# Two query tiles taken through the chunks as they are normalized, and token rows moved behind the queries

## The chip, the cores and the metric

The kernel runs on one core of a Trainium2 chip. The metric is the device time of one execution in microseconds; three runs of the kernel before were timed. Engines: TensorE (PE; PEld is its weight load), VectorE (DVE), ScalarE (ACT), GpSimd (POOL) and SyncE (SP), which here only issues transfers.

## What is computed

One decoder layer over 512 tokens of width 2048, in float32:

```
xn = rmsnorm(x, norm_mix);  proj = xn @ w_in            # 80 tiles of 128 columns
y_conv = (gated 3-tap convolution) @ w_conv_out
y_attn = stick-breaking attention (16 heads of 64) @ w_attn_out
x = x + (sigmoid(g_conv)*y_conv + sigmoid(g_attn)*y_attn) @ w_out
xn = rmsnorm(x, norm_ffn)
q = xn @ peer_wq                                        # 16 tiles of 128 columns
scores = q . subkeys; top 16 of each half; top 16 of the sums -> 128 experts a token
x = x + sum_k gelu(xn . u[k]) * gate[k] * v[k]
out = rmsnorm(x, norm_final)
```

## The kernel before

**Precision.** Each product of two float32 operands is made of three matmuls: both operands are split into a high part (`whi`, ScalarE, L130) and a low part (`wlo`, VectorE, L131), and `mm3` (L160) adds high·high, high·low and low·high. Weights come as halves of 128x1024 (`whalf`, L139): a transfer by SP into one of four raw buffers, then a split into one of three high and three low buffers. The pace of TensorE is therefore tied to one split on ScalarE and one on VectorE for each half.

**Halves.** The tokens are taken in two halves of 256 (h = 0 and 1): projections, attention and gates (`mixer`), then the output projection with the residual (`outproj`, L450), then the second norm (`chain`, L490), then the queries (`queries`, L527). The expert part of the first 192 tokens is done row by row: for each of 128 slots a token row of u is fetched with an indirect transfer on POOL (`fetch`, L690) and multiplied on VectorE (L701, 128x2048), later the same with v (L708). The other 320 tokens are done densely against all 16384 experts (`dense`), which is most of the second half of the time.

**outproj** has two column halves of eight steps `kp`; each step takes two weight halves for both token tiles. After a column half, VectorE adds the residual (L483) and ScalarE squares the sum (L484), once for each of the two token tiles.

**chain** makes the norm's factor of each token tile (`rms_inv`: L194 adds the two sums, L195 takes the root on ScalarE, L196 inverts), spreads it over the partitions (L498, a matmul at L499, L502), and then goes through eight chunks of two 128-column blocks each: four transposes (`turn`, L205), two scalings on VectorE (L508), and a split into high and low parts of the normalized x (`yhi`/`ylo` in the first half, `dxhi`/`dxlo` in the second). In the first half it then also makes the token rows that the row-by-row part needs: it loads the gain row, scales both token tiles in place (L517, 128x2048) and stores them, and stores the part of x that the dense stage needs. In the second half it loads that part back.

**queries** computes 16 tiles: 48 matmuls each, a copy (L536) and two small products with the sub-keys (L538). In the second half it begins in the program when `chain` has ended.

**Order.** The program is written with generators: work on the side (routing, one-hot gates, row fetches) is advanced between the steps of the main work by `background` (L965) with a rate per step; `pump` (L911) issues that many rows. A planner then orders the instructions of each engine by a timeline of its own, so an instruction that is ready early may move ahead of earlier ones. `keep_in_program_order` forbids one instruction to move ahead of what was traced before it on its engine; the products at L701 and L708 are pinned so. An output step that yields "end" is not given side work (only the last step of the second half in the kernel before); `pump(SKIPEND * RATE_O)` then issues 1.6 rows after the chain. PSUM has three banks named `pj` (accumulators, also used by the transposes), two double banks `z`, and one bank `tr`.

Of the kernel before, what the change touches and what calls it, by code (L numbers as in the profile page):

```python
# [53 lines left out]
XKB = 3  # L54
# [26 lines left out]
def block_kernel(ctx, tc, a, out, dbg=None):  # L81
# [117 lines left out]
    def turn(x2, k, pin):  # L199

        tp = accum()
        for kk in range(2):
            for tt in range(2):
                o = kk * NH + tt * P
                t = nc.tensor.transpose(tp[:, o:o + P], x2[tt][:, (k + kk) * P:(k + kk) * P + P], ident)  # L205
                if pin:
                    behind(t)
        return tp.rearrange("p (k t) -> p k t", k=2)
# [241 lines left out]
    def outproj(pool, h, m, box):  # L450
# [5 lines left out]
        for half in range(2):  # L456
            zt = [ztile() for _ in range(2)]
            for kp in range(8):
# [16 lines left out]
                if half == 1 and kp == 7 and h:  # L475
                    if PRE1:
# [4 lines left out]
            for tt in range(2):  # L481
                hs = slice(half * 1024, half * 1024 + 1024)
                nc.vector.tensor_tensor(x2[tt][:, hs], zt[tt], x2[tt][:, hs], OP.add)  # L483
# [6 lines left out]
    def chain(pool, h, box, nhi, nlo, c0):  # L490

        x2 = box["x2"]
        ib = accum()
# [8 lines left out]
        nc.scalar.copy(inv, ib[:, 0:NH])  # L502
        yield
        for k in range(0, KD, 2):
            tp = turn(x2, k, h == 0 and PINT)
# [3 lines left out]
            split(xk, nhi[:, k:k + 2, c0:c0 + NH], nlo[:, k:k + 2, c0:c0 + NH])  # L509
            yield  # L510
        if h == 0:
            grow = row()
            nc.sync.dma_start(grow, a["norm_ffn"].broadcast_to([P, D]))
            yield
            for tt, rn in enumerate(rns):
                xn = x2[tt]
                nc.vector.scalar_tensor_tensor(xn, xn, rn, grow, OP.mult, OP.mult)  # L517
                stop = min(tt * P + P, G0)
                nc.sync.dma_start(xn2d[tt * P:stop], xn[0:stop - tt * P])
                yield  # L520
            nc.sync.dma_start(ntd[0], nhi[:, :, G0:].bitcast(F32))
            nc.sync.dma_start(ntd[1], nlo[:, :, G0:].bitcast(F32))
        else:
# [3 lines left out]
    def queries(pool, h, st, nhi, nlo, c0):  # L527

        for half in range(2):
            zt = [ztile() for _ in range(2)]  # L530
            for cg in range(8):
                ct = half * 8 + cg
                acc = accum()[:, :NH]
                yield from mmk(acc, wtile(a["wq"][ct]), lambda k: nhi[:, k, c0:c0 + NH], lambda k: nlo[:, k, c0:c0 + NH])
# [451 lines left out]
    for what in queries(sm, 0, st, *n0, 0):  # L986
        background("half", 0)
    for what in ahead:
# [7 lines left out]
    with tc.tile_pool(name="cp", bufs=1, side="right") as cp:  # L996
        for _ in chain(cp, 1, box[1], *st["dense_x"], ND - NH):
            pass
# [3 lines left out]
    for what in queries(sm, 1, st, *st["dense_x"], ND - NH):  # L1002
# [94 lines left out]
```

## Time and profile before

| | us |
|---|---|
| median of three runs | 3612.64 (3610.05 to 3616.29) |
| profiled execution | 3619.12 |
| its span | 3617.4 |
| TensorE busy | 3513.1 |
| VectorE busy | 2831.2 |
| ScalarE busy | 1616.3 |
| POOL busy | 659.3 |

The span is what the profile covers of the profiled execution. Starts are microseconds from its beginning. In a timeline row, the first two numbers are start and duration, and a bracket at the end gives how long the engine was idle before the instruction and whose end released it. In a row of stretches, each engine has its busy time and, in brackets, its number of instructions; PEclk is the granted clock of TensorE (1.00 is 2.4 GHz, 0.50 is 1.2 GHz). The names of the tiles: `z` and `pj` are PSUM, `row` a token row of 128x2048, `wlo`/`whi` split weights, `sg` a scaled chunk, `ssq` the sums of squares.

### The profile page before, as it was taken

Reading aid. Unit: us, or ns where it says so; the run is one execution under the profiler, and the core shown is the slowest. Engines: PE = TensorE matmul, PEld = TensorE weight load, DVE = VectorE, ACT = ScalarE, POOL = GpSimd, SP = SyncE. Lnnn points to the kernel's source line nnn. Section 1 sums busy time; section 2 is a strip of 40 time slices with the busy share of each in tenths; the row PEclk is TensorE's granted clock in tenths of the full one; section 3 lists DMA queues with packets and bytes.
Section 4 is the critical chain, followed back from the end, with each engine's and each line's share of the span. In section 5 each row is a group of like instructions: output and inputs, shape, how many; then the busy total and the mean of one; then the engine's idle time right before and its main releaser. Section 6 shows DMA issues by size and latency. Waiting matters only on the chain.

```text
span 3617.4 us, 63262 instructions
## 1 busy us (share of the span) xinstructions
PE 3513.1 (97%) x25347; PEld 3410.4 (94%) x25347; DVE 2831.2 (78%) x4022; ACT 1616.3 (45%) x2275; POOL 659.3 (18%) x520
## 2 busy tenths in 40 slices
PE   9999999999999999889999999999999999999998
PEld 8999998898888999779999999999999999999998
DVE  6565557559987878788999886888887878888886
ACT  6454445445555534544337773333333333333334
POOL 0000000001233322112131111221122322322220
PEclk9999999999999999999999999999999999999999
DMA  6556555654788889898888889899988988899884
GB/s 204 180 178 225 187 187 196 208 184 137 260 348 309 335 332 346 322 331 335 298 327 319 311 315 365 329 356 338 339 328 328 346 330 333 327 346 343 328 329 162
DMA packets 292920, 1049.29 MB, mean 290 GB/s; under 512 B 35921, under 2 KB 105169, under 8 KB 238673
## 3 DMA queue, kind: packets, MB, share of 16 engines
q1 hardware_dynamic: 237328, 642.56, 50.5%
q0 software_dynamic: 55296, 402.68, 28.7%
q8 instruction: 199, 3.26, 0.4%
q14 instruction: 97, 0.79, 0.1%
HBM read 996.57 MB, written 47.97 MB: 289 GB/s over the span
## 4 chain that ended last, share of the span: by engine, by line
PE 59%; DMA 5%; DVE 4%; issue 2%; ACT 1%; POOL 0%; SPq 0%; ACTq 0%; DVEq 0%; POOLq 0%
PE pj L163 10%; PE pj L161 10%; PE pj L162 10%; PE z L161 9%; PE z L162 9%; PE z L163 9%; DVE wlo L131 2%; DMA wraw<-in_w_in 2%; PE pj L673 2%; DMA row<-in_u,idx 1%; DVE row L701 1%; ACT whi L130 1%; PE z L439 1%; DMA row<-in_v,idx 0%; DMA wraw<-in_w_mix 0%
## 5 line engine op out<-in xcount | busy, mean ns | idle before, releaser
L130 ACT ACTIVATE whi<-wraw 128x1024 fp32r<-128x1024 f32 x827 | 874.1, 1059 | 1258.0 <-PE pj L162 723.2
L131 DVE TENSOR_TENSOR wlo<-wraw,whi 128x1024 fp32r<-128x1024 f32 x827 | 1008.3, 1223 | 412.5 <-ACT whi L130 405.6
L161 PE MATMUL pj<-xhi,whi 128*128 128x256 f32 x2560 | 723.5, 283 | 12.5 <-ACT whi L130 10.3
L163 PE MATMUL pj<-xhi,wlo 128*128 128x256 f32 x2560 | 720.4, 283 | 13.5 <-DVE wlo L131 13.4
L162 PE MATMUL pj<-xlo,whi 128*128 128x256 f32 x2560 | 718.1, 281 | 0.0
L161 PE MATMUL pj<-dxhi,whi 128*128 128x320 f32 (+1 forms) x2304 | 710.0, 308 | 4.5 <-ACT whi L130 4.3
L163 PE MATMUL pj<-dxhi,wlo 128*128 128x320 f32 (+1 forms) x2304 | 703.6, 307 | 3.4 <-DVE wlo L131 3.3
L162 PE MATMUL pj<-dxlo,whi 128*128 128x320 f32 (+1 forms) x2304 | 705.2, 306 | 0.0
L161 PE MATMUL z<-ahi,whi 128*128 128x320 f32 x2048 | 632.0, 310 | 3.9 <-ACT z L190 2.9
L162 PE MATMUL z<-alo,whi 128*128 128x320 f32 x2048 | 631.8, 309 | 2.4 <-DVE alo L131 2.4
L163 PE MATMUL z<-ahi,wlo 128*128 128x320 f32 x2048 | 630.6, 309 | 1.8 <-DVE wlo L131 1.8
L163 PEld LDWEIGHTS pj<-xhi,wlo 128*128 128x128 f32 x2560 | 481.6, 189 | 23.6 <-DVE wlo L131 20.9
L161 PEld LDWEIGHTS pj<-xhi,whi 128*128 128x128 f32 x2560 | 482.5, 188 | 21.1 <-ACT whi L130 14.4
L690 POOL DMA_INDIRECT row<-in_v,idx x192 | 292.7, 1525 | 1060.2 <-DVE row L708 429.8
L162 PEld LDWEIGHTS pj<-xlo,whi 128*128 128x128 f32 x2560 | 482.3, 188 | 2.8 <-issue 1.6
L708 DVE SCALAR_TENSOR_TENSOR row<-row,gact 128x2048 f32<-128x2048 f32 x192 | 450.3, 2345 | 27.2 <-DMA row<-in_v,idx 27.2
L701 DVE SCALAR_TENSOR_TENSOR row<-row,gx 128x2048 f32<-128x2048 f32 x192 | 438.3, 2286 | 31.2 <-DMA row<-in_u,idx 31.1
L690 POOL DMA_INDIRECT row<-in_u,idx x192 | 289.0, 1505 | 863.1 <-DVE row L701 239.9
L161 PEld LDWEIGHTS pj<-dxhi,whi 128*128 128x128 f32 x2304 | 434.3, 189 | 5.5 <-ACT whi L130 5.1
L163 PEld LDWEIGHTS pj<-dxhi,wlo 128*128 128x128 f32 x2304 | 432.9, 188 | 5.4 <-DVE wlo L131 5.4
L162 PEld LDWEIGHTS pj<-dxlo,whi 128*128 128x128 f32 x2304 | 434.0, 188 | 0.0
L130 ACT ACTIVATE whi<-spare 128x1024 fp32r<-128x1024 f32 x197 | 208.8, 1060 | 425.4 <-PE z L162 266.9
(232 smaller groups left out, 4979.8 us busy)
## 6 DMA issues: line engine op xcount, KB each, us to landing
wraw<-in_w_in SPq DMA_DIRECT2D x320, 512.0 KB
wraw<-in_uT SPq DMA_DIRECT2D x187, 512.0 KB
wraw<-in_vT SPq DMA_DIRECT2D x128, 512.0 KB
spare<-in_vT SPq DMA_DIRECT2D x128, 512.0 KB
spare<-in_uT SPq DMA_DIRECT2D x69, 512.0 KB
wraw<-in_w_mix SPq DMA_DIRECT2D x64, 512.0 KB
wraw<-in_w_out SPq DMA_DIRECT2D x64, 512.0 KB
wraw<-in_wq SPq DMA_DIRECT2D x64, 512.0 KB
```

Source lines behind the costliest of these rows:

```text
L130: nc.scalar.activation(hi, src, AF.Copy)
L131: nc.vector.tensor_tensor(lo, src, hi.bitcast(F32), OP.subtract)
L161: nc.tensor.matmul(acc, shi, mhi, start=first, stop=False)
L162: nc.tensor.matmul(acc, shi, mlo, start=False, stop=False)
L163: pe_last[0] = nc.tensor.matmul(acc, slo, mhi, start=False, stop=last)
L439: nc.tensor.matmul(z[:, c], stat.bitcast(F32), src[:, c], start=False, stop=True, skip_group_check=True)
L673: behind(nc.tensor.matmul(gp[:, t * P:t * P + P], oh[:, t, 0], oh[:, t, 1], start=True, stop=True))
L690: ins = nc.gpsimd.indirect_dma_start(out=g, out_offset=None, in_=tab, in_offset=bass.IndirectOffsetOnAxis(ap=idx[0:np_, s:s + 1], axis=0))
L701: pin(nc.vector.scalar_tensor_tensor(g, g, 1.0, gx, OP.mult, OP.mult, accum_out=hid[:, s:s + 1]))
L708: pin(nc.vector.scalar_tensor_tensor(acc[0:np_], g, act[:, s:s + 1], acc[0:np_], OP.mult, OP.add))
```

## The change

1. The second half's queries are given the chain as a generator. They take two accumulators and, for each chunk that the chain has normalized, run the matmuls of the first two query tiles on that chunk; weight halves are requested for both tiles at a time. Then they go on as before from the third tile.
2. In the second half the transposes are made two chunks ahead, the first two before the norm's factor; they alternate between a `pj` bank and the bank `tr`, and the norm's spread uses a `z` bank.
3. The last four output steps of the second half (`CALM = 4`) yield "end", so no rows and no side work are issued there; at the last one ScalarE's square root table is loaded ahead. The two residual adds of the last column half are pinned in program order.
4. In the first half, the token rows, their stores and the store of the dense part leave `chain` for `norm_rows`, which is advanced while the queries run (after the first, fourth and sixth yield); the two scalings are pinned there.
5. The second half's scaled chunk has two buffers for three (`XKB`).

```diff
+CALM = 4
-XKB = 3
+XKB = 2
-    def turn(x2, k, pin):
-        tp = accum()
+    def turn(x2, k, pin, bank=None):
+        tp = accum() if bank is None else bank
...
-                if half == 1 and kp == 7 and h:
-                    if PRE1:
+                if half == 1 and kp >= 8 - CALM and h:
+                    if kp == 7:
                         tc.keep_in_program_order(nc.scalar.preload_act_table_set("sqrt_and_others"))
                     yield "end"
...
-                nc.vector.tensor_tensor(x2[tt][:, hs], zt[tt], x2[tt][:, hs], OP.add)
+                add = nc.vector.tensor_tensor(x2[tt][:, hs], zt[tt], x2[tt][:, hs], OP.add)
+                if h and half:
+                    tc.keep_in_program_order(add)
...
-        ib = accum()
+        tps = {}
+        def ahead_turn(k):
+            if k < KD:
+                bank = trtile() if h and k % 4 else None
+                tps[k] = turn(x2, k, h == 0 and PINT, bank)
+        if h:
+            ahead_turn(0)
+            ahead_turn(2)
+        ib = ztile() if h else accum()
...
         for k in range(0, KD, 2):
-            tp = turn(x2, k, h == 0 and PINT)
+            if h == 0:
+                ahead_turn(k)
+            tp = tps.pop(k)
...
             split(xk, nhi[:, k:k + 2, c0:c0 + NH], nlo[:, k:k + 2, c0:c0 + NH])
+            if h:
+                ahead_turn(k + 4)
             yield
...
+    def norm_rows(box, nhi, nlo):
+        nc.sync.dma_start(ntd[0], nhi[:, :, G0:].bitcast(F32))
+        nc.sync.dma_start(ntd[1], nlo[:, :, G0:].bitcast(F32))
+        grow = row()
+        nc.sync.dma_start(grow, a["norm_ffn"].broadcast_to([P, D]))
+        yield
+        for tt, rn in enumerate(box["rns"]):
+            xn = box["x2"][tt]
+            tc.keep_in_program_order(nc.vector.scalar_tensor_tensor(xn, xn, rn, grow, OP.mult, OP.mult))
+            stop = min(tt * P + P, G0)
+            nc.sync.dma_start(xn2d[tt * P:stop], xn[0:stop - tt * P])
+            yield
+    def queries(pool, h, st, nhi, nlo, c0, ch=None):
+        if ch is not None:
+            two = [accum()[:, :NH] for _ in range(2)]
+            next(ch)
+            for c in range(2):
+                ws = [whalf(a["wq"][ct, c]) for ct in range(2)]
+                for k in range(8 * c, 8 * c + 8):
+                    if k % 2 == 0:
+                        next(ch)
+                    for acc, (whi, wlo) in zip(two, ws):
+                        b = slice(k % 8 * P, k % 8 * P + P)
+                        mm3(acc, whi[:, b], wlo[:, b], nhi[:, k, c0:c0 + NH], nlo[:, k, c0:c0 + NH], k == 0, k == KD - 1)
+            for _ in ch:
+                pass
+            yield "two"
...
-    for what in queries(sm, 0, st, *n0, 0):
+    rest = norm_rows(box[0], *n0)
+    for i, what in enumerate(queries(sm, 0, st, *n0, 0)):
         background("half", 0)
+        if i in (0, 3, 5):
+            next(rest)
...
-        for _ in chain(cp, 1, box[1], *st["dense_x"], ND - NH):
-            pass
+        second = queries(sm, 1, st, *st["dense_x"], ND - NH, chain(cp, 1, box[1], *st["dense_x"], ND - NH))
+        next(second)
```

## Rows read from the trace of the kernel before

**Rows 1.** The page's busy time, share of the span and instructions, TensorE.
```profile
PE 3513.1 (97%) x25347; PEld 3410.4 (94%) x25347; DVE 2831.2 (78%) x4022; ACT 1616.3 (45%) x2275; POOL 659.3 (18%) x520
```

**Rows 2.** Busy time by stretch: stretch, length, engines, granted clock, share of DMA, GB/s.
```profile
730.00:812.00 82.00, 82.00 (x702) 82.00 (x702) 43.38 (x98) 35.43 (x46) 0.00 (x0) 1.00 0.53 173
...
1540.00:1590.60 50.60, 49.96 (x231) 40.54 (x230) 36.31 (x47) 25.50 (x37) 8.39 (x6) 1.00 0.93 348
1590.60:1607.30 16.70, 7.11 (x38) 5.49 (x37) 14.97 (x28) 9.49 (x17) 2.68 (x2) 0.80 1.03 331
...
1620.00:1712.00 92.00, 92.00 (x766) 92.00 (x765) 78.59 (x124) 37.63 (x48) 24.61 (x15) 1.00 0.92 347
...
2900.00:3000.00 100.00, 100.00 (x684) 100.00 (x683) 83.03 (x86) 35.99 (x45) 25.11 (x17) 1.00 0.87 333
```

**Rows 3.** Timeline of TensorE, last output matmul to first query matmul.
```profile
1590.21 0.39 PE L163 MATMUL z<-whi,xlo 128*128 128x512 f32 x1
...
1603.11 0.63 PE L205 MATMUL pj<-ident,row 128*128 128x128 f32 x4 [0.22 <-DVE sg L508]
1605.10 0.63 PE L205 MATMUL pj<-ident,row 128*128 128x128 f32 x4 [1.36 <-DVE sg L508]
...
1607.27 0.36 PE L161 MATMUL pj<-dxhi,whi 128*128 128x256 f32 x1 [0.15 <-DVE sg L508]
```

**Rows 4.** Timeline of VectorE in the second half's chain.
```profile
1590.62 1.22 DVE L131 TENSOR_TENSOR wlo<-wraw,whi 128x1024 fp32r<-128x1024 f32 x1
1591.75 1.22 DVE L483 TENSOR_TENSOR row<-z,row 128x1024 f32<-128x1024 f32 x1
1592.89 2.28 DVE L701 SCALAR_TENSOR_TENSOR row<-row,gx 128x2048 f32<-128x2048 f32 x1
...
1595.09 0.15 DVE L194 TENSOR_TENSOR ssq<-ssq 128x1 f32<-128x1 f32 x1
...
1598.64 0.16 DVE L196 RECIPROCAL ssq<-ssq 128x1 f32<-128x1 f32 x1
1600.53 2.44 DVE L508 SCALAR_TENSOR_TENSOR sg<-pj,gffn,cinv 128x256 f32<-128x256 f32 x6 [1.73 <-ACT cinv L502]
...
1610.41 1.47 DVE L131 TENSOR_TENSOR dxlo<-sg,dxhi 128x512 fp32r<-128x512 f32 x2
```

**Rows 5.** Timeline of ScalarE in the second half's chain and queries.
```profile
1593.00 1.03 ACT L484 ACTIVATE z<-row 128x1024 f32<-128x1024 f32 x1 [0.17 <-DVE row L483]
...
1594.17 1.28 ACT L195 ACT_TABLE_LOAD   x1
...
1596.48 0.29 ACT L195 ACTIVATE ssq<-ssq,epst 128x1 f32<-128x1 f32 x1 [0.72 <-DVE ssq L194]
...
1598.83 0.40 ACT L498 ACTIVATE rb<-ones,ssq 128x128 f32<-128x128 f32 x1 [1.76 <-DVE ssq L196]
...
1601.43 0.63 ACT L130 ACTIVATE dxhi<-sg 128x512 fp32r<-128x512 f32 x1 [0.94 <-DVE sg L508]
...
1626.54 0.35 ACT L536 COPY pq<-pj 128x256 f32<-128x256 f32 x1
...
1632.74 0.35 ACT L536 COPY pq<-pj 128x256 f32<-128x256 f32 x1
```

**Rows 6.** Busy time by stretch, second half's chain, for the granted clock.
```profile
1594.00:1595.00 1.00, 0.00 (x0) 0.00 (x0) 1.00 (x1) 0.98 (x3) 0.00 (x0) 0.72 1.24 260
...
1601.00:1607.00 6.00, 3.54 (x24) 2.36 (x22) 6.00 (x15) 3.15 (x5) 0.00 (x0) 0.98 1.00 408
```

**Rows 7.** Timeline of TensorE, end of the first half's chain.
```profile
710.48 0.39 PE L162 MATMUL pj<-ylo,whi 128*128 128x256 f32 x1 [1.82 <-DVE ylo L131]
...
712.50 0.35 PE L161 MATMUL pj<-yhi,whi 128*128 128x256 f32 x1 [1.16 <-DVE sg L508]
```

**Rows 8.** Timeline of VectorE, end of the first half's chain.
```profile
705.22 4.61 DVE L517 SCALAR_TENSOR_TENSOR row<-row,ssq 128x2048 f32<-128x2048 f32 x2
709.75 0.68 DVE L131 TENSOR_TENSOR ylo<-sg,yhi 128x512 fp32r<-128x512 f32 x1
```

More of the change, by code (lines that the diff above doesn't have):

```diff
@@ L502, in chain @@
         nc.scalar.copy(inv, ib[:, 0:NH])
+        box["rns"] = rns
         yield
         for k in range(0, KD, 2):
-            tp = turn(x2, k, h == 0 and PINT)
+            if h == 0:
+                ahead_turn(k)
+            tp = tps.pop(k)
             xk = pool.tile([P, 2, NH], F32, name="sg", bufs=1 if h == 0 else XKB)
@@ L509, in chain @@
             split(xk, nhi[:, k:k + 2, c0:c0 + NH], nlo[:, k:k + 2, c0:c0 + NH])
+            if h:
+                ahead_turn(k + 4)
             yield
[L511 to L523, printed above, removed]
+        if h:
             nc.sync.dma_start(nhi[:, :, 0:c0].bitcast(F32), ntd[0])
             nc.sync.dma_start(nlo[:, :, 0:c0].bitcast(F32), ntd[1])
-    def queries(pool, h, st, nhi, nlo, c0):
+    def norm_rows(box, nhi, nlo):
[25 more added lines that the diff above has]
+            yield "two"
         for half in range(2):
@@ L532, in queries @@
                 ct = half * 8 + cg
-                acc = accum()[:, :NH]
-                yield from mmk(acc, wtile(a["wq"][ct]), lambda k: nhi[:, k, c0:c0 + NH], lambda k: nlo[:, k, c0:c0 + NH])
+                if ch is not None and ct < 2:
+                    acc = two[ct]
+                else:
+                    acc = accum()[:, :NH]
+                    yield from mmk(acc, wtile(a["wq"][ct]), lambda k: nhi[:, k, c0:c0 + NH], lambda k: nlo[:, k, c0:c0 + NH])
                 pq = pool.tile([P, NH], F32, name="pq", bufs=2)
@@ L984, in background @@
             pump(rate)
-    for what in queries(sm, 0, st, *n0, 0):
+    rest = norm_rows(box[0], *n0)
+    for i, what in enumerate(queries(sm, 0, st, *n0, 0)):
         background("half", 0)
+        if i in (0, 3, 5):
+            next(rest)
+    for _ in rest:
+        pass
     for what in ahead:
@@ L1001, in block_kernel @@
     st["scp"] = small.enter_context(tc.tile_pool(name="scp", bufs=1))
-    for what in queries(sm, 1, st, *st["dense_x"], ND - NH):
+    for what in second:
         background(what, RATE_Q)
```

## Prediction

> **What bounds the kernel now.** I read the page first: TensorE is busy for 97% of the span [rows 1], so time can only be won where TensorE stands idle or is waiting on one chain, and everything else is cover. The busy time by stretch then says where that is. Once the last two thirds are running it is 100.00 of 100 us, with VectorE at 83% beside it; the two stretches that the change touches are not like that [rows 2]. In the last 50.6 us of the second output projection TensorE lacks only 0.6 us, so there is nothing to be had inside it. In the 16.7 us behind it TensorE works 7.1 us and VectorE 15.0.
>
> The timelines say why. Second half: TensorE's last output matmul ends at 1590.6 and the first query matmul starts at 1607.27 [rows 3]. VectorE in between is in a queue of its own making [rows 4]: the second residual add waits behind a weight split (1590.62) and starts only at 1591.75, and two token-row products of 2.28 us stand ahead of the root-mean-square steps: L194 of the first token tile runs only at 1595.09, when the first product ends, and L196 of the second at 1598.64, when the other one ends. On ScalarE a table load of 1.28 us lies in the same place [rows 5]. The first chunk's scaling starts at 1600.53. First half: the chain there is hidden beside projections, but TensorE waits 1.82 and 1.16 us for the sixth and seventh chunk [rows 7], since two token-row scalings (L517, together 4.61 us at 705.22) run ahead of the sixth chunk's low part at 709.75 [rows 8].
>
> **The change, part by part.** All sums are made against the profiled execution, 3619.12 us with a span of 3617.4; the median of the three timed runs is 3612.64, so I work out a difference there and take it from the median.
>
> *First half: token rows behind the queries.* L517 no longer stands ahead of the chunks, since it is issued after the second and third query tile and pinned there. VectorE then does the sixth chunk's low part at 705.2 instead of 709.75, the seventh chunk by 708.1 and the eighth by 709.5 (about 0.8 for its two scalings, 0.63 for the high part, 0.68 for the low one [rows 4, 5, 8]). TensorE needs them at 708.7, where it stopped, and then one each 0.7 us. Both waits go: **3.0 us**. The next wait would be the second weight half's low part, split at 708.9 to 710.1 once VectorE is free, and covered by the remaining chunks. In its new place L517 stands in a stretch where VectorE works 43 of 82 us and TensorE is never idle; products of the same length already stand in the second half's queries at no TensorE idle time (92.00 of 92) [rows 2]. So 0 there; without that cover 4.6. The two stores to the dense rows and the gain row's load move with it, behind the last chunk on SP's queue, where they also stood before; the weight loads queued behind them are four buffers ahead. I take 0. Bounds: -1 (the planner puts other filler there, and more of it) to 3.0 us, all that was idle.
>
> *Second half: no gathers in the last four output steps.* Three steps more than before issue no row (the last one issued none already), 2.4 rows at 0.8 a step. A product runs one or two steps of 5.6 us behind its request, so with none requested in the last 22 us the two products in the chain, 2 x 2.28, are gone. Table load: issued at the last output step, in a stretch where ScalarE works half of the time (25.5 of 50.6 [rows 2]), so 1.28 is hidden; if not, it stands before the square root as it does now. I follow the chain with the intervals of before. Add of the second token tile ends at 1592.9 (I leave the weight split ahead of it, since no pin forbids it). The square and its read-out take 1.16 (1593.00 to the table load at 1594.17); then come L194 (0.15), the square root (0.29) and L196 (0.16), with 0.1 to 0.2 of handing over before each: some 2.05 from the start of the square to the broadcast. From the broadcast (1598.83) to the first scaling (1600.53) it is 1.70 [rows 4, 5]. First scaling: 1593.05 + 2.05 + 1.70 = 1596.8, **3.7 us earlier**. Without the split ahead of the add it would be 1595.7.
>
> *Second half: two query tiles with the chunks.* Scaling to high part is 0.90, the high part 0.63, the low part behind it 0.7: the first chunk is usable at about 1599.0. From there TensorE owes two query tiles, 6.20 us each (from one query copy to the next [rows 5], the small sub-key products in it), and transposes: eight of the 32 run ahead in the wait for the norm and four more before the first chunk is split; the other twenty are five groups of 0.63 [rows 3]. 1599.0 + 12.4 + 3.15 = 1614.55. VectorE is not later: eight chunks took 11.35 us (1600.53 to 1611.88), and with three weight splits of 1.22 it is done at 1611.8 [rows 4]. Two things I add. The granted clock: some 3.7 us into the idle time it fell to 1.2 GHz, and from 1601 on it was 2.4 again [rows 6]. If the same happens now, the matmuls from 1599.0 to about 1601.6 go at half speed: 1.3 us (0 to 2). And the weight buffers: three are there for four halves, so the fourth is converted only when the first is free, 1.06 + 1.22 of conversion against 0.7 of the other tile's matmuls and 0.63 of transposes: 1.0 us. End of both tiles 1616.85. Before it is 1607.27 + 12.4 = 1619.67. **2.8 us gained**, less than the 3.7 that the norm gains, because before the queries of the first tile already started before the last two chunks were done. Bounds: +6.2 (no split ahead of the add, no clock loss, no buffer wait) to the loss under the rivals.
>
> *What is put off.* The 2.4 rows come later, in the even pacing of the long last stage: 2.4 x 2.36 = 5.7 us of VectorE spread over some 1300 us where TensorE lacks nothing [rows 2]. I take 0; the whole 5.7 if that cover were gone. The smaller edits (two buffers for the scaled chunk for three, the broadcast in another PSUM pool, the pinned adds) move no work; 0 each, with -1 to +1 for what they do to the planner's order.
>
> Sum: 3.0 + 2.8 = 5.8 us; 3617.4 - 5.8 = 3611.6 of span, and from the median 3612.64 - 5.8 = **3606.8 us**.
>
> **A rule against it.** In the second half's old chunk loop TensorE worked in bursts of 0.63 us with idle time of 0.22 to 1.36 between them (59% busy from 1601 to 1607 [rows 3, 6]), and the granted clock stayed at 1.00. The Trainium skill (TensorE: Matmul & The Clock Gate, section "HAM oscillation — how this bites in real kernels") says that matmul bursts shorter than the waits between them leave the clock throttled in each burst anew. By that the new loop would stay at half clock and the sum would become a loss (third rival); the trace speaks against it, since its bursts were sparser than those to come.
>
> **The rivals.**
> 1. *The chunk loop hides nothing.* The loop is paced by VectorE, ScalarE and the three weight buffers, so that the two tiles end where they ended, at 1619.7. For it: VectorE has 15 us of work in the stretch and the four weight splits now fall among the chunks. Against: the sum of its work ends at 1611.8. Only the first half's 3.0 remains: 3609.6.
> 2. *Everything fits.* The adds run back to back, and neither clock nor buffers cost anything: 6.2 + 3.0 = 9.2, 3603.4. For it: the pinned adds stand next to each other in the text. Against: the weight split that came between them can be ready as early as before, and the idle time after 1590.6 is still there for the clock.
> 3. *The other side: the chunk loop runs at half clock from end to end.* Place: TensorE between the norm and the end of the second tile. Price: 12.4 + 3.15 becomes 31.1, so that it ends at 1599.0 + 31.1 + 1.0 = 1631.1 against 1619.7, 11.4 lost, less 3.0 from the first half: 8.4 slower, 3621.0. It decides from the point where the clock takes 7.1 us (1619.67 - 1614.55 - 1.0 + 3.0), that is 14.2 us at 1.2 GHz; below that the change still gains. Against it stand the rows just named.
> A change that does nothing would need L517 and the products to be put back into the same places by the planner; the pins and the missing requests exclude most of that, and I count it with the first rival.
>
> **How the numbers follow.** Forecast 50% (its own range 3603.5 to 3609), first rival 20%, second 20%, third with everything else that makes it slower 10%. A difference under 0.2% (7.2 us) can't be told from none here, so faster starts below 3605.4: four tenths of the forecast's share and nearly all of the second rival's, 0.20 + 0.18 = 0.38; slower starts above 3619.9, half of the third: 0.06; the rest, 0.56, is no change that can be told. The range goes from 3600 (the second rival with 3 us of planner luck) to 3616 (half of the third rival's loss).
>
> **What would show it.** Right: in the changed trace no token-row product (2.28 us) on VectorE from the last output matmul to the end of the second query tile; the first scaling some 6 us after that matmul instead of 10; two query accumulators alternating between transposes, ending some 26 us after it instead of 29; no table load between the last square and the square root; L517 among the query weight splits and no TensorE wait over 1 us from 705 to 715. Wrong: granted clock at 0.5 for most of the chunk loop; TensorE waiting on the low part of each chunk or on the fourth weight half for several us; a weight split waiting behind L517; or new TensorE idle time elsewhere of several us, which would mean that the planner's new order and not these steps decides.

## The result: slower by half a percent, and the profile after

The changed kernel takes 3631.55 us (3628.06 to 3634.73) beside 3613.74 us for the kernel before: 1.0051 times as long, 95% interval 1.0040 to 1.0061, that is 17.8 us slower. I had forecast 5.8 us faster. Its profiled execution took 3633.94 us, with a span of 3632.3.

I cut the span at marks that both traces have: the last matmul of each output projection, the copies of the query tiles (L536 before, L574 after) and the activations of the dense tiles. "Again" is a second profile of the kernel before; E16 is the last but one experiment below. Lengths in us, worked out from the traces:

| stretch | before | again | changed | E16 |
|---|---|---|---|---|
| to the end of the first output projection | 678.4 | 681.3 | 678.8 | 680.2 |
| to the first query copy, first half | 40.3 | 40.1 | 36.9 | 37.0 |
| to the last one | 87.8 | 87.8 | 86.2 | 86.2 |
| to the end of the second output projection | 784.1 | 783.4 | 786.3 | 782.7 |
| of it that projection itself | 103.7 | 103.7 | 109.3 | 104.9 |
| to the second query copy, second half | 29.7 | 29.7 | 30.1 | 30.3 |
| to the last one | 85.9 | 85.9 | 95.2 | 86.3 |
| to dense tile 8 | 65.0 | 65.0 | 67.9 | 66.1 |
| to dense tile 16 | 60.5 | 60.5 | 65.0 | 63.5 |
| to dense tile 63 | 399.3 | 399.5 | 395.1 | 392.9 |
| to dense tile 127 | 1310.7 | 1309.5 | 1315.4 | 1309.4 |
| to the end | 75.6 | 75.6 | 75.4 | 75.4 |

The 5 us won in the first half are there, but the second output projection, the queries, the dense tiles up to 16 and the down stages (dense tile 63 to 127) are 27 longer together (the projection's 5.6 only in part a loss, see E3), of which the stretch in between gives back 4. One caution: both profiles of the kernel before lie some 6 us above its median, and in four kernels below whose text differs only from the last output steps on (E4, E5, E6, E9), the whole stretch to the end of the second projection took 775 to 778 us. That row therefore decides nothing. The projection alone repeats to 0.1 us in the kernels without part 4 of the change, but what it has more in those with it has to be taken apart (E3).

Against [rows 1] and [rows 2]: TensorE's busy time on the page of the changed kernel, then its stretches (columns as in rows 2). The queries (from 1617.6) are no longer full, and the stretch behind the output matmuls has a clock of 0.70 where it had 0.80.

```profile
PE 3522.3 (97%) x25347; PEld 3417.8 (94%) x25347; DVE 2831.5 (78%) x4022; ACT 1615.7 (44%) x2275; POOL 676.9 (19%) x520
```
```profile
730.00:812.00 82.00, 82.00 (x695) 81.51 (x694) 46.71 (x122) 37.91 (x47) 0.00 (x0) 1.00 0.54 179
...
1588.20:1605.00 16.80, 10.19 (x59) 9.87 (x59) 11.56 (x24) 7.95 (x15) 0.00 (x0) 0.70 0.66 188
...
1592.00:1601.00 9.00, 6.16 (x27) 5.87 (x28) 6.15 (x14) 3.89 (x9) 0.00 (x0) 0.50 0.93 287
...
1617.60:1709.60 92.00, 85.40 (x682) 84.22 (x683) 74.61 (x122) 32.86 (x42) 27.23 (x15) 0.96 0.83 307
2900.00:3000.00 100.00, 100.00 (x684) 100.00 (x683) 80.38 (x84) 35.12 (x44) 27.43 (x17) 1.00 0.88 341
```

VectorE in the chain, against [rows 4]: no product between the adds and the norm, and the first scaling 6.2 us behind the last output matmul (1588.23) instead of 9.9. But for the fifth chunk it waits for transposes.

```profile
1589.37 1.22 DVE L484 TENSOR_TENSOR row<-z,row 128x1024 f32<-128x1024 f32 x1
...
1594.47 0.88 DVE L524 SCALAR_TENSOR_TENSOR sg<-pj,gffn,cinv 128x256 f32<-128x256 f32 x2 [1.96 <-ACT cinv L515]
...
1602.64 0.88 DVE L524 SCALAR_TENSOR_TENSOR sg<-pj,gffn,cinv 128x256 f32<-128x256 f32 x2 [2.23 <-PE pj L206]
```

TensorE there, against [rows 3] and [rows 6]: two waits of 4.57 and 2.03 us, then matmuls of 0.41 us that start 0.21 us apart; from 1601.6 on they are of 0.28, 0.12 apart.

```profile
1592.80 1.22 PE L512 MATMUL z<-ident,rb 128*128 128x128 f32 x4 [4.57 <-ACT rb L511]
1596.06 0.79 PE L162 MATMUL pj<-dxhi,whi 128*128 128x256 f32 x2 [2.03 <-ACT dxhi L131]
...
1597.71 0.41 PE L164 MATMUL pj<-dxhi,wlo 128*128 128x256 f32 x1
...
1601.89 0.28 PE L164 MATMUL pj<-dxhi,wlo 128*128 128x256 f32 x1
```

Then come the queries. VectorE does three products back to back, and a later one stands waiting 2.57 us for its row while three weight splits queue behind it:

```profile
1612.82 2.28 DVE L739 SCALAR_TENSOR_TENSOR row<-row,gx 128x2048 f32<-128x2048 f32 x1
...
1615.03 2.29 DVE L739 SCALAR_TENSOR_TENSOR row<-row,gx 128x2048 f32<-128x2048 f32 x1
...
1617.25 2.29 DVE L739 SCALAR_TENSOR_TENSOR row<-row,gx 128x2048 f32<-128x2048 f32 x1
...
1629.95 2.29 DVE L739 SCALAR_TENSOR_TENSOR row<-row,gx 128x2048 f32<-128x2048 f32 x1 [2.57 <-DMA row<-in_u,idx]
...
1632.17 3.49 DVE L132 TENSOR_TENSOR wlo<-wraw,whi 128x1024 fp32r<-128x1024 f32 x3
```

TensorE waits for the low part behind it, and is at half clock for the next 6 us:

```profile
1620.73 0.38 PE L164 MATMUL pj<-dxhi,wlo 128*128 128x256 f32 x1 [1.32 <-DVE wlo L132]
...
1633.44 0.58 PE L164 MATMUL pj<-dxhi,wlo 128*128 128x256 f32 x1 [2.90 <-DVE wlo L132]
```

POOL shows where the rows come from. A fetch is released by a query copy, and with two tiles taken together there is no such copy until 1617.08; the fetches then follow each other:

```profile
1609.51 1.43 POOL L728 DMA_INDIRECT row<-in_u,idx  x1 [0.30 <-issue]
1617.70 2.65 POOL L728 DMA_INDIRECT row<-in_u,idx  x1 [6.76 <-ACT pq L574]
1620.65 3.04 POOL L728 DMA_INDIRECT row<-in_u,idx  x1 [0.30 <-issue]
```

### The profile page after: what moved, and what is told of

It is laid out like the page before. It is cut to its first block, busy times and chain, and to the rows that moved or that the text cites. A ratio compares the mean times of both kernels' runs of the same rounds, so it can differ in the third digit from the quotient of the medians.

```text
span 3632.3 us, 63261 instructions
## 1 busy us (share of the span) xinstructions
PE 3522.3 (97%) x25347; PEld 3417.8 (94%) x25347; DVE 2831.5 (78%) x4022; ACT 1615.7 (44%) x2275; POOL 676.9 (19%) x520
## 5 line engine op out<-in xcount | busy, mean ns | idle before, releaser
L728 POOL DMA_INDIRECT row<-in_u,idx x192 | 303.5, 1581 | 878.7 <-DVE row L739 199.8
```

What stands on the lines that cost most here:

```text
L728: ins = nc.gpsimd.indirect_dma_start(out=g, out_offset=None, in_=tab, in_offset=bass.IndirectOffsetOnAxis(ap=idx[0:np_, s:s + 1], axis=0))
```

## The experiments

Each is given with its time, the kernel before run beside it (3610.7 to 3613.8 us), and the ratio with its 95% interval. "Row waits" are VectorE's waits for a row's transfer from 1585 to 1850 us, from the view of waits.

**E1, no burst.** Changed kernel; the first two query tiles issue no row.

```diff
-                yield
+                yield "half" if ch is not None and ct < 2 else None
```


> The changed kernel, but the yields of the two tiles that went through with the chunks are marked as half steps, so that no token row is issued at them (in the changed kernel 1.6 + 1 + 1 rows are issued there with no matmul in between). Theory A, the burst: seven products stood on VectorE from 1612.8 to 1637.8 ahead of weight splits, and TensorE lost 6.5 us between the second and the fifth query copy; without them it loses under 2, so 6 to 9 us less than the changed kernel: 3623 to 3626. Theory B, the rows put off: they are late anyway and meet the routing's work on VectorE in the dense stage (7 us lost there); four rows are late now instead of two, so that loss stays, and the total stays within 3 us of 3631. Theory C, the chunk loop at half clock is what costs: no change, 3631.

3636.02 us, ratio 1.0068 (1.0049 to 1.0086), above what any of the three theories expected. The queries take 86.2 us instead of 95.2, and the dense tiles to the eighth 64.1 instead of 67.9: that is what the burst costs in this order. But the total is no better, because the rows now lie four behind those of the kernel before (124 fetches by dense tile 8 for 128; 126 in the changed kernel), and the last gathered tile's norm falls into the last down stage. TensorE stands there until ScalarE, which writes the squares into a `z` bank, is done with it; first TensorE, then ScalarE:

```profile
3552.60 0.64 PE L162 MATMUL z<-ahi,whi 128*128 128x320 f32 x1 [7.07 <-ACT z L191]
```
```profile
3551.40 1.03 ACT L191 ACTIVATE z<-row 128x1024 f32<-128x1024 f32 x1 [2.75 <-DVE row L801]
```

**E2, rows issued again in three of the quiet output steps.** Changed kernel.

```diff
-CALM = 4
+CALM = 1
```


> The changed kernel with rows issued again in three of the four last output steps (CALM = 1), the rest as changed. Theory A: the burst behind the two tiles stays (1.6 + 1 + 1), so the 6.5 us stay, and the norm is later by up to 3.7 us since products stand in the chain again: 3630 to 3635. Theory B: no row is late, so the 7 us in the dense stage go: 3622 to 3626. Theory C: 3631 or a little more.

3631.17 us, 1.0050 (1.0034 to 1.0066): no change. The queries lose 2.3 instead of 9.3 us, the down stages 0.3 instead of 4.7, but dense tiles 8 to 63 lose 9.3 instead of 0.3.

**E3, token rows behind the first half's queries, alone.** Part 4 of the change on the kernel before, nothing else.

```diff
+    rest = norm_rows(box[0], *n0)
+    for i, what in enumerate(queries(sm, 0, st, *n0, 0)):
...
+        if i in (0, 3, 5):
+            next(rest)
...
```


> The kernel before with only the first half's token rows, their stores and the dense part's store moved behind the chain into the queries. All theories: the query copies of the first half come 4.5 us earlier as in the changed kernel, and nothing gives that back: 3609 (3.5 to 5 us under before). If the planner's new order downstream is what decides, it is anywhere from 3604 to 3620.

3624.29 us, 1.0027 (1.0018 to 1.0036). The part with the surest gain is a loss by itself. It does win 5.1 us up to the last query copy. Behind it, it is longer in the second output projection (4.9), up to the second query copy (1.7), and in dense tiles 8 to 16 (3.3) and 16 to 63 (1.4). The projection took 103.6 to 103.7 us in all eight profiles of kernels without this part and 107.1 to 110.7 in eight with it (the four with it that come to 104.8 or 104.9 are further down). TensorE of the changed kernel there, and VectorE just before:

```profile
1496.40 0.50 PE L163 MATMUL z<-wlo,xhi 128*128 128x512 f32 x1 [1.85 <-DVE wlo L132]
```
```profile
1492.91 2.28 DVE L739 SCALAR_TENSOR_TENSOR row<-row,gx 128x2048 f32<-128x2048 f32 x1
1495.12 0.08 DVE L739 DVE_READ_ACCUMULATOR row<-row,gx 128x1 f32 x1
1495.12 2.36 DVE L132 TENSOR_TENSOR wlo<-wraw,whi 128x1024 fp32r<-128x1024 f32 x2
```

A product lies ahead of two splits, and its row is there: it had waited for none. The wait is 1.85 us, and the granted clock behind it stays at 1.00. The projection's time at half clock (0.50) lies at its start, behind another wait, which the kernel before has too, but one projection tile earlier, so that its half clock falls outside this cut. TensorE before, then after, with the stretches at half clock behind the wait, and the one behind the wait of 1.85 us:

```profile
1480.19 0.58 PE L161 MATMUL pj<-yhi,whi 128*128 128x256 f32 x1 [9.56 <-ACT whi L130]
```
```profile
1480.20:1485.20 5.00, 4.54 (x19) 4.24 (x20) 3.72 (x4) 2.11 (x2) 0.00 (x0) 0.50 1.00 386
```
```profile
1477.63 1.22 PE L162 MATMUL z<-whi,xhi 128*128 128x512 f32 x2 [8.21 <-ACT whi L131]
```
```profile
1478.90:1482.30 3.40, 3.40 (x8) 2.72 (x9) 2.97 (x3) 1.65 (x3) 0.00 (x0) 0.50 0.63 192
...
1496.40:1503.00 6.60, 6.60 (x33) 5.53 (x34) 6.60 (x11) 1.95 (x4) 2.06 (x2) 1.00 0.95 307
```

So the changed kernel's 5.6 us more are, by my estimate from these rows, 1.7 of half clock that has only moved across the cut, 1.2 for twelve transposes that now run ahead (by as much E13, E14, E16 and E17 are longer, which have no such waits), and some 2.3 of waits that are new; 0.4 are left over. Only the new waits are shown to be a loss.

**E4, quiet output steps, table load and pinned adds, alone.** Part 3 on the kernel before.

```diff
+CALM = 4
...
-                if half == 1 and kp == 7 and h:
+                if half == 1 and kp >= 8 - CALM and h:
...
```


> The kernel before with only the four calm output steps, the square root table loaded ahead and the pinned adds; the chain and the queries as before. The first scaling comes some 3.7 us earlier behind the last output matmul. Theory A (the burst needs the two tiles taken together): the gain of about 3.5 us stays, 3609 to 3611. Theory B (2.4 rows late meet the routing): 7 us are lost in the dense stage, 3616 to 3618. Theory C: 3610.

3630.76 us, 1.0048 (1.0033 to 1.0063), again above all three expectations. It loses 7.8 us from dense tile 8 to 16 and, with its 2.4 late rows, 4.7 in the down stages.

**Control: the kernel before once more**, no edit.

> The kernel before once more, unchanged, for a second profile of it and for what two sets of executions of one program differ by. Theory N (an order that the kernel before has and all others lose): dense tiles 8 to 16 take 60.5 us here too, the second half's output projection 104 us from its first matmul to its last, and the ratio is 1.000 within 0.001. If the first profile only caught a lucky execution there, the stretch takes 64 to 69 us here as in the variants. The 9.56 us wait of TensorE for a weight half ahead of the second output projection in the first profile is missing, as it is in the profiles of the three variants that share the program up to there: span some 6 us shorter, 3611.

3613.69 us, 1.0004 (0.9995 to 1.0013). Its stretches repeat to 0.2 us from the second projection to dense tile 63, and to 1.2 in the next one. So the losses elsewhere belong to the programs, not to the execution. I had expected the 9.56 us wait ahead of the second projection to be missing; it is there again (9.38), so that was wrong.

**E5, the lag alone.** The kernel before, with 2.4 rows fewer requested behind the chain.

```diff
-        pump(SKIPEND * RATE_O)
+        pump(SKIPEND * RATE_O - 2.4)
```


> The kernel before, with 2.4 token rows fewer requested at one place (behind the second half's chunks, -0.8 for 1.6 in the count of rows), and nothing else: no rows behind the queries, no query tiles with the chunks, no quiet output steps. All later rows are 2.4 later in the row order, as in the changed kernel. Theory L (the lag of the rows itself costs): the stretch from dense tile 63 to 127 takes 1315.4 us instead of 1310.7, with the two squares of the first gathered tile's norm (ScalarE, into the z banks) at the second down stage's products instead of just before them; total 3 to 6 us over before. Theory B (only the burst of rows in the first query tiles costs): no longer than before, within 2 us either way, since this kernel has no burst and less VectorE work in the queries. The stretch from dense tile 8 to 16 tells a third thing: 60.5 us as before, if what is lost there in all variants needs another program order; 64 to 68 if a lag alone does it.

3623.15 us, 1.0032 (1.0021 to 1.0043). Less work at one place, and 10 us slower. The down stages take 1314.6 us instead of 1310.7, as the lag theory wants; dense tiles 8 to 16 take 64.6, and the row waits are 20.5 us.

**E6, two chunk buffers for three, alone**, and **E9, the table load alone**, each on the kernel before.

```diff
-XKB = 3
+XKB = 2        # E6
-PRE1 = 0
+PRE1 = 1       # E9
```


> The kernel before with two buffers for the scaled chunk for three, the smallest edit of the change alone; it moves no work and no row. Theory N (any new order out of the planner loses what the kernel before has): 3 us or more slower than before, and some of it between dense tiles 8 and 16. Theory L or B (named places cost, the order by itself does not): same as before within 2 us, dense tiles 8 to 16 in 60 to 61 us, dense tiles 63 to 127 in 1311.

> The kernel before with one thing of the change alone: the square root's table is loaded at the last output step. It removes 1.28 us from ScalarE in the norm and touches no row, buffer or weight. Theory of named places: the first scaling of the second half comes 0 to 1.3 us earlier, all later stretches are as before, 3611 to 3613. Theory N: at least 3 us slower than before, lost in stretches behind the norm that this edit does not touch (dense tiles 8 to 16 in 63 us or more).

E6: 3626.32 us, 1.0039 (1.0026 to 1.0053). E9: 3629.86 us, 1.0046 (1.0033 to 1.0059). Two edits that touch no row cost 14 and 16 us, which speaks for the theory of orders. The view of waits suggested one mechanism for it. VectorE's waits for a row (in all, times, longest) in the kernel before again, the changed kernel, E6 and E9:

```profile
DVE row L701 <- DMA row<-in_u,idx: 2.1, 4, 1.3
```
```profile
DVE row L739 <- DMA row<-in_u,idx: 14.0, 7, 3.8
```
```profile
DVE row L701 <- DMA row<-in_u,idx: 14.2, 8, 2.8
```
```profile
DVE row L701 <- DMA row<-in_u,idx: 15.6, 9, 2.9
```

VectorE in E9: the product waits 2.93 us, and three splits are done only behind it.

```profile
1626.34 2.29 DVE L701 SCALAR_TENSOR_TENSOR row<-row,gx 128x2048 f32<-128x2048 f32 x1 [2.93 <-DMA row<-in_u,idx]
1628.56 0.08 DVE L701 DVE_READ_ACCUMULATOR row<-row,gx 128x1 f32 x1
1628.56 3.49 DVE L131 TENSOR_TENSOR wlo<-wraw,whi 128x1024 fp32r<-128x1024 f32 x3
```

Every kernel but the one before has these waits: with those for rows of v, 6.0 to 20.5 us in the changed kernel and E1 to E11, against 3.6 and 2.3 in the two profiles of that one. They follow the time only roughly: 6.0 to 9.4 us in E3, E8, E10, E11 (3623 to 3625), 10 to 17 in the seven from E6's 3626 up to E1's 3636, and 20.5 in E5, which is an exception at 3623. The later runs break the rule altogether: 0.6 us in E15 (3627), 5.8 to 7.1 in E12, E13 and E14 (3625 to 3635). So these waits are a part of the cost, and not its measure.

**E7 and E8, no burst, and the lag made up** in the first eight down stages (E7) or in the other fourteen query tiles (E8). Both on E1.

```diff
-RV = 0.9
+RV = 0.945     # E7
-RATE_Q = 1.0
+RATE_Q = 1.314 # E8
```


> The changed kernel without the burst (the first two query tiles issue no row, so that the rows lie 4.4 behind those of the kernel before), and with the lag made up in the down stages of the first eight chunks (the factor on the even pacing there 0.945 for 0.9). Theory L: the last gathered tile's norm leaves the last down stage (the 7.07 us wait for a z bank goes) and the first one's stands again before the ninth down stage (6.87 us wait becomes some 2.9), so 11 to 14 us less than the same kernel with the lag (3636.0): 3622 to 3625. Theory N: the loss stays, 3630 or more, at other places.

> The same kernel without the burst, the lag made up in the other fourteen query tiles (1.314 rows a tile for 1.0), so that the rows stand where they stand in the kernel before from the dense stage on. Theory L: from the dense stage on nothing is lost to late rows (dense tiles 63 to 127 in 1311 us, end 75.6 us after the last one), and the queries keep most of the 5.4 us that they were ahead if VectorE has room for 1.3 products a tile: 3610 to 3620. Theory N: the loss between dense tiles 8 and 16 and elsewhere stays, 3625 or more. If VectorE has no room in the query tiles, they end 5 us later than without the catching up, with TensorE waits on weight halves' low parts there.

E7: 3628.98 us, 1.0052 (1.0038 to 1.0066), 7 less than E1 and 4 above the end of what the lag theory expected: the norm has left the last stage (75.4 us), but the down stages now take 1319.6. E8: 3624.88 us, 1.0031 (1.0020 to 1.0043): the down stages are back at 1310.0 and dense tiles 8 to 16 at 59.1, as the lag theory says, but the queries take 92.9 us and the next eight dense tiles 70.5. VectorE has no room for 1.3 products a tile.

**E10, the changed kernel with three chunk buffers, and E11, with no burst too (as E1) and the rows issued earlier.**

```diff
-XKB = 2
+XKB = 3        # E10, E11
-RATE_A2 = 0.85
+RATE_A2 = 0.935 # E11
```


> The changed kernel with three buffers for the scaled chunk for two. Theory: the third scaling no longer waits for the first chunk's low part, so that the second query copy comes 0 to 2 us earlier; the burst of rows and the lag stay as they are: 3628 to 3632. Theory N: by another order alone 5 us or more to either side, at places that have no chunk in them.

> The changed kernel with three such buffers, no rows from the first two query tiles (no burst), and the missing 4.4 rows issued ahead of the output projection, by 0.935 rows a step for 0.85 in some 52 steps of the second half's mixer. Theory of named places: no burst (-12), no lag (-4.7), so 3613 to 3618, the second output projection's 5.8 us and the dense tiles 8 to 16 being all that is lost; the queries end 5 us earlier than in the kernel before's first profile. Theory N: 3625 or more.

E10: 3623.01 us, 1.0026 (1.0016 to 1.0036), 8.5 less than the changed kernel, all of it outside the chunks: second query copy at 30.1 us as in the changed kernel, queries 86.1 instead of 95.2. Its first three products are back to back as well, so a burst by itself is not enough to do the harm. E11: 3624.39 us, 1.0030 (1.0020 to 1.0039): queries 83.4, down stages 1309.5, as expected, but dense tiles 8 to 63 lose 13.5.

**E12 to E15, fetches released one mark earlier.** In the second profile of the kernel before a row takes 7.6 us from issue to landing (median of 14 in the queries), and a query tile 6.2; in the changed kernel 7.9. The edit lets a fetch go one copy sooner. E12 has it on E9, E13 on the changed kernel, E14 on it with three buffers and no burst, E15 on the kernel before.

```diff
-LAG = 1
+LAG = 2
```


> The kernel before with the table load moved (which alone made it 16 us slower), and each row fetch released by the query or projection copy one step earlier (a lag of two marks for one), so that a row is there some 6 us sooner. Theory W (VectorE's pinned products stand ahead of weight splits and wait for rows that have not landed: 15.6 us in nine waits from 1585 to 1850 against 2 to 3 us in the kernel before): these waits fall under 6 us and the time comes back to 3613 to 3620. Theory N (another order costs by itself, the waits are a sign of it): 3625 or more, whatever the waits do.

> The changed kernel with the earlier release of the fetches alone. Theory W: waits of VectorE for rows from 1585 to 1850 fall from 15.2 us to under 6; what is left of the loss is the lag of the rows (4.7), the second output projection (5.8), and two buffers for the scaled chunk: 3620 to 3626. Theory N: 3628 or more.

> The changed kernel with three remedies: earlier release of the fetches, three buffers for the scaled chunk, no rows from the first two query tiles. The lag of 4.4 rows stays, with the last gathered norm inside the last down stage (7 us). Theory W: 3618 to 3626 (the version with neither of the first two was at 3636.0). Theory N: 3630 or more.

> The kernel before with the earlier release of the fetches alone, the control for the other three. Theory W: it waits for rows for 2 to 3 us only in that stretch, so little is to be won there (27 us of such waits lie in the mixer and 26 in the dense up stages, where they cost TensorE little): 3608 to 3615. Theory N: 3620 or more, since the order is another one.

E12: 3626.08 us, 1.0036 (1.0023 to 1.0049). E13: 3625.39 us, 1.0037 (1.0024 to 1.0050). E14: 3634.82 us, 1.0066 (1.0053 to 1.0079). E15: 3627.04 us, 1.0041 (1.0027 to 1.0055). By total time three of the four miss the waiting theory. By stretches it holds where it speaks. In E12 the row waits fall from 15.6 to 5.9 us, and against E9 the queries go from 91.4 to 85.9, dense tiles 8 to 16 from 65.1 to 60.5, and the next stretch from 404.2 to 394.3. In E13 the queries go from 95.2 to 86.2 and the second projection from 109.3 to 104.8 (there VectorE waited for no row; the long wait at its start is back ahead of the cut, and the one of 1.85 us is gone, in this order). What takes it back is the down stages: 1317.4 to 1320.5 us in all four, also in E15. E14 adds the 4.4 late rows, with 7.5 us at the very end. One place in the down stages is the same in all four: a product that now comes early stands ahead of a split, where in the kernel before the split comes first, and TensorE waits 4.02 us there (4.01 in E14) instead of 1.75, with half clock behind it. VectorE, then TensorE, in E15:

```profile
2259.81 2.34 DVE L708 SCALAR_TENSOR_TENSOR row<-row,gact 128x2048 f32<-128x2048 f32 x1
2262.07 1.22 DVE L131 TENSOR_TENSOR wlo<-spare,whi 128x1024 fp32r<-128x1024 f32 x1
```
```profile
2263.34 0.63 PE L163 MATMUL z<-ahi,wlo 128*128 128x320 f32 x1 [4.02 <-DVE wlo L131]
```

**E16 and E17, both places mended.** Changed kernel, earlier release only up to the first down stage, and the 2.4 late rows made up in the first 64 dense tiles; E17 has three chunk buffers besides.

```diff
-RATE_W = 1.0
+RATE_W = 1.0375
+    lag = [2]
...
-            if len(anchors) > LAG:
-                tc.add_manual_dep(ins.ins, anchors[-1 - LAG].ins.name, ...
+            if len(anchors) > 2:
+                tc.add_manual_dep(ins.ins, anchors[-1 - lag[0]].ins.name, ...
...
                 side = None
+                lag[0] = LAG
-XKB = 2
+XKB = 3        # E17
```


> The changed kernel with fetches released one step earlier up to the first down stage only (from there on as in the kernel before, since the earlier release cost 8 to 11 us there in all four kernels that had it), and the 2.4 late rows made up in the first 64 dense tiles (1.0375 rows a tile for 1.0). Theory W with the lag: dense tiles 63 to 127 in 1310 us instead of 1320, so 11 us less than the changed kernel with the earlier release everywhere (3625.4): 3612 to 3617, level with the kernel before. Theory N: 3622 or more, the loss turning up elsewhere.

> The same with three buffers for the scaled chunk for two, which was worth 8.5 us on the changed kernel. Theory of named places: where the waits for rows are gone already, the third buffer gives at most the 1 to 2 us of the chunk loop: 3609 to 3616, the one version here that could be faster than the kernel before. Theory N: 3622 or more.

E16: 3614.63 us, 1.0008 (0.9999 to 1.0017). E17: 3615.07 us, 1.0004 (0.9995 to 1.0013). Both are as expected level with the kernel before, and some 16 us faster than the changed kernel; neither can be told from the kernel before. The row waits of E16 (u and v) over 1585 to 1850:

```profile
DVE row L740 <- DMA row<-in_u,idx: 3.3, 2, 2.5
...
DVE row L747 <- DMA row<-in_v,idx: 1.8, 1, 1.8
```

The loss is thus a sum of places that could be mended here, and in these two it did not come back elsewhere. That another order, by luck, would have done the same is not ruled out: E15 has hardly a row wait left and is at 3627. With the waits gone, the third buffer, worth 8.5 us in E10, is worth nothing, which fits: what it gave in E10 lay outside the chunks. The two edits of E16 were not tried apart.

## Why the prediction was wrong

**First half, 3.0 us: right there, and lost later.** L517's successor runs among the weight splits (first at 709.23), and TensorE has no wait over 1 us from 705 to 715, against [rows 7] and [rows 8]. The gain is 5.0 us at the last query copy, above my bound of 3.0: the kernel before has 3.4 us at half clock up to its first query copy (0.50 from 696.7 to 700.1; in its second profile from 713.4 to 716.9), the changed kernel none (1.00 from 690 to 720), which is worth 1.7 and which I had not counted. The step that fails is the zero that I put on the scalings' new place: I looked at the stretch where they went (82.00 of 82 again), not at the order that the planner makes further on. Alone (E3) it won 5.1 us, and yet its program is 11 us slower: 2.7 us of new waits in the second output projection (1.85 and 0.84), 1.7 up to the second query copy, and 4.7 in dense tiles 8 to 63 go against it; the rest is not placed, since the mixer's time differs by 6 us and more from one execution to the next.

**Norm 3.7 us earlier: right to the tenth.** First scaling 6.24 us behind the last output matmul against 9.93. The split stayed ahead of the second add, and the table load was hidden, at 1581.17 with VectorE and TensorE busy.

**Chunk loop, 2.8 us: nothing; the first rival.** The second query copy comes 30.1 us behind the last output matmul, against 29.7. I had the eight chunks done 15 us after the first scaling; they took 18.4. The half clock lasts to 1601.6 as I assumed, yet it cost more than the 1.3 us: the fifth chunk's transposes stand in TensorE's queue behind half-speed matmuls of two tiles, and VectorE waits for them (2.23 us at 1602.64). That the loop is a circle, TensorE to VectorE to ScalarE and back, was missing in a sum that ran the engines side by side. Two of my signs failed with it: the two tiles end 30 us behind the last output matmul and not 26, and token-row products run from 1612.82 on, before the second tile's copy.

The third rival fell: the clock was back at 1.00 from 1602 on, with waits of 0.28 and 0.69 us still to come. The rule of the Trainium skill (TensorE: Matmul & The Clock Gate, section "HAM oscillation — how this bites in real kernels") that I had weighed against the change speaks of matmul bursts shorter than the waits between them. This loop was not of that kind: behind the wait of 2.03 us at 1596.06 TensorE worked on to the end of the loop with no wait over 0.7, so the trace does not test the rule as a whole. Idle time answered by half clock it does show, and at more places than I had looked at: at the 2.90 us wait at 1633.44 too. (In the chances, half of the third rival's 10% is 0.05 and not 0.06.)

**What is put off, 0, and the smaller edits, 0 with 1 either way: the steps that failed.** With the scalings' new place they cost the loss. The prices do not add up: alone, part 3 (E4), part 4 (E3) and part 5 (E6) are 18, 11 and 14 us slower, and all together 18.
1. The first query copy comes 28.9 us behind the last output matmul (24.3 before), and the row requests of two tiles are held until then and come together. In this order that cost 9.3 us in the queries and 2.9 after them. E1 takes it away, and E13 most of it; but so does E10, which keeps the burst, so the burst costs only together with this order.
2. 2.4 rows later means that products meet other weight splits and other `z` banks in the down stages: 4.7 us, 4.7 in E4 and 3.9 in E5, gone in E16. I had spread their 5.7 us of VectorE time over 1300 us where TensorE lacks nothing. But it is not VectorE's sum that counts. In the changed kernel three of its waits there lie behind products or the norm's squares (TensorE; the kernel before has the middle one too, 2.86 us, and in place of the first 0.61):

```profile
2654.97 0.56 PE L162 MATMUL z<-ahi,whi 128*128 128x320 f32 x2 [1.91 <-ACT ahi L131]
...
2769.54 0.63 PE L162 MATMUL z<-ahi,whi 128*128 128x320 f32 x1 [2.44 <-ACT z L191]
...
3119.05 0.41 PE L164 MATMUL z<-ahi,wlo 128*128 128x320 f32 x1 [2.07 <-DVE wlo L132]
```
3. Two buffers and the moved table load "move no work", and cost 14 and 16 us alone. They change which product stands at the head of VectorE's queue. At some places its row has not landed. I had read that a product runs one or two steps behind its request, and never asked for the row's landing time, 7.6 us against a tile of 6.2. It is the price of a wait that the kernel before hardly shows (2 to 4 us), and which every edit from E1 to E11 brought out. At other places the rows have landed, and two products stand ahead of a split that in the kernel before ran between them (below). That the two forms together make up the whole 14 and 16 us is not shown.

I had named "the planner's new order" as what would make the prediction wrong, and priced it at 1 us. Its price here is 10 to 16.

## What stays open

Dense tiles 8 to 16 take 63.5 us in E16, where VectorE hardly waits for rows any more, against 60.5; E12 and E15 have 60.5 and 60.4 with the kernel before's text in the first half. The traces name the instructions: two products and a reduction stand in one piece ahead of a split, no product waits for its row, and TensorE waits for the low part and is then at half clock. VectorE in the changed kernel, then TensorE there and in E16, and E16's clock behind its wait:

```profile
1797.99 2.31 DVE L739 SCALAR_TENSOR_TENSOR row<-row,gx 128x2048 f32<-128x2048 f32 x1
...
1801.33 2.30 DVE L739 SCALAR_TENSOR_TENSOR row<-row,gx 128x2048 f32<-128x2048 f32 x1
...
1803.54 1.24 DVE L132 TENSOR_TENSOR wlo<-wraw,whi 128x1024 fp32r<-128x1024 f32 x1
```
```profile
1804.84 0.63 PE L164 MATMUL pj<-dxhi,wlo 128*128 128x320 f32 x1 [2.75 <-DVE wlo L132]
```
```profile
1807.88 0.41 PE L165 MATMUL pj<-dxhi,wlo 128*128 128x320 f32 x1 [1.54 <-DVE wlo L133]
```
```profile
1808.30:1811.60 3.30, 3.30 (x14) 3.30 (x14) 3.30 (x9) 0.00 (x0) 0.34 (x1) 0.50 1.03 251
```

In the kernel before a split runs between these products, at 1792.61, and TensorE's waits there are at most 1.0 us, with no half clock. What stays open there is why the planner puts them so, and whether an order without such places could be had on purpose: no run sets this order alone. In the down stages an earlier release costs 8 to 11 us, of which the place in E12 to E15 named above accounts for some 4 to 5 (2.3 of wait, and 1.6 to 2.6 of half clock behind it, by my estimate); the rest was not placed. And parts 1 and 2, the query tiles with the chunks, were never run without parts 3 to 5.

## What to carry to other kernels

Where an engine's in-order queue holds work pinned behind a transfer, compare the transfer's time from issue to landing with the time between request and use before anything else: if they are close, an edit upstream can turn the margin into waits for whatever is queued behind. And see what stands directly behind such work: in these traces a product whose row was there delayed the split behind it, and TensorE, all the same. Price such an edit by what it does to margin and order, not by the work that it moves. And when a tuned kernel gets slower all over, cut both traces at common marks and repeat the old kernel's profile: the stretches that repeat to a tenth tell which losses are real.

## What the runs showed of the hardware that I had not expected

Row transfers of 128 rows of 8 KB took 7.6 us in the median from issue to landing in the queries of the kernel before (its second profile), and 8.8 in E9's, beside the same weight transfers. Executions of one program differ little by stretch (0.2 us between two profiles from the second projection to dense tile 63, 1.2 in the down stages) except further ahead, where TensorE has its long waits for weight halves: the same mixer and second projection took 775 to 784 us. And a wait of TensorE did not always cost its own length alone: the one of 2.90 us at 1633.44 was followed by 5.9 us of matmuls at half clock, which cost as much again, and that of 1.54 us at 1807.88 in E16 by 3.4 us of them; behind the one of 1.85 us at 1496.40 the clock stayed at 1.00.
